# Adding a half-deep third chunk to the seven-product gate and up strips of a two-layer decoder kernel

## The chip, the cores and the metric

The kernel runs on one core of a Trainium2 chip. The metric is device time in microseconds (us) of one execution, lower is better. Engines are named as the profile names them: PE is TensorE (matrix products), DVE is VectorE, ACT is ScalarE, POOL is GpSimd, SP is the engine whose queue issues the transfers.

## The reference, cut to what matters

Two decoder layers on 256 tokens of width 2048, all in 32-bit floats. The change touches the feed-forward part of each layer, with `h` of 256 x 2048 and gate and up weights of 2048 x 5632:

```
h = rms_norm(x, pre_ffn_gain[i])
f = (jax.nn.silu(h @ w_ffn_gate[i]) * (h @ w_ffn_up[i])) @ w_ffn_down[i]
x = x + rms_norm(f, post_ffn_gain[i])
```

## The kernel before, in words

Every product with a weight matrix is made exact enough by splitting both factors into a high and a low part: weights arrive as "raw" chunks `wr` of 256 rows x 512 columns (tile 128x2x512, 512 KB), ACT casts a chunk to its high part `wh` (line 305), DVE subtracts to get the low part `wl` (line 315), and PE does three matmuls of 128x512 for each 128 rows and each 128 tokens: activation high and low against `wh`, activation high against `wl` (lines 404, 407, 408, in function `acc`). There are two token blocks, so one chunk feeds 2 x 2 x 3 = 12 matmuls. The pool of `wh` and `wl` has 7 tiles of each kind, the pool of raw chunks 10. A tile is given out again when its last reader is done.

A strip is 512 output columns, eight chunks deep (2048 rows). The gate strip and the up strip of the same columns are computed together in `paired`. For the first two chunks `fast` treats the two token blocks by the two chunks by the two strips as a 2 x 2 by 2 x 2 block product and forms it from seven products instead of eight (Winograd's variant of Strassen's scheme), with sums of activation blocks made once in a layer (`mixed`) and differences of weight chunks made on DVE in place (line 420). The running sums sit in PSUM tiles: `u` (a tile of the pool `ms`), `c`, `e`, `a` and `d` (`accc`, `acce`, `acca`, `accd`). In the order of the program the seven products are: `u` with chunk r11, then a copy of `u` to SBUF; `c`; `e` with r21; `a`; after the first plain chunk `second` adds to `u`; after the last plain chunk of the gate strip `third` adds to `c` and to `u`. The other six chunks of each strip follow as `plain` chunks: six of gate into `e` and `a`, then six of up into `c` and `d`. When a strip is done DVE adds the saved pieces (lines 381 and 452), ACT takes Silu, DVE multiplies (line 1145), transposes 32x32 blocks (line 251) and the result goes through DRAM to come back turned, after which it is split into `ck` tiles (lines 203 and 204).

Each layer has eleven gate and up strip pairs, numbered n = 0 to 10. The pair n = 0 runs as two ordinary strips, the ten others through `paired`, so there are twenty such pairs in the program. They alternate with the down products in groups of 2, 3, 3 and 3 hidden strips: pairs n = 1 and 2, down group 0, n = 3 and 4, down group 1, n = 5 to 7, down group 2, n = 8 to 10, down group 3. A down pair also goes through `paired`, with four chunks (group 0) or six. Before each down group `mixed` makes sums of the hidden activations (lines 367 and 373).

Each engine executes its instructions in the order that a scheduler fixed when the program was built; a tile's slot and every wait are fixed then too.

Of the kernel before, what the change touches and what calls it, by code (L numbers as in the profile page):

```python
# [15 lines left out]
P = 128  # L16
SEQ = 256
NT = 2
# [29 lines left out]
def decoder(ctx: ExitStack, tc: tile.TileContext, x, p, positions, w_in, attn_sinks,  # L48
# [18 lines left out]
    def tiny(n):  # L67
        return sm.tile([P, n], F32, tag="tiny", name="tiny", bufs=16)
# [4 lines left out]
    def later(n, fn):  # L73

        queue.append((clock[0] + n, fn))
# [19 lines left out]
    def tick():  # L95
        clock[0] += 1
        for gen in list(running):
            if next(gen, True):
                running.remove(gen)
        for item in [q for q in queue if q[0] <= clock[0]]:  # L100
            queue.remove(item)
            item[1]()

    def nat(shape=(P, W), dt=F32):
        return np_.tile(list(shape), dt, tag="nat", name="nat")
# [35 lines left out]
    G.memset(mhalf, -0.5)  # L141


    g0rows = cp.tile([32, P], F32, name="g0rows")
    S.dma_start(g0rows, pre_mix_gain.rearrange("l (c p) -> (l c) p", p=P))
    gT = cp.tile([P, P], F32, name="gT")
    busy = bank()
# [6 lines left out]
    T.transpose(ps[:, 0:32], g0rows, ident[0:32, 0:32])  # L154
    S.preload_act_table(AF.Copy)
    first = V.tensor_copy(gT[:, 0:32], ps[:, 0:32])
    grows = cp.tile([96, P], F32, name="grows")
    lrows = cp.tile([16, P], F32, name="lrows")
    lbl = cp.tile([P, DEPTH, 8], F32, name="lbl")

    at = 0
# [135 lines left out]
    def fetch_w(w, c, col):  # L297
        raw = wpr.tile([P, 2, W], F32, tag="wr", name="wr")
        nc.sync.dma_start(raw, w[c * 2 * P:(c + 1) * 2 * P, col:col + W].rearrange(
            "(k p) n -> p k n", p=P))  # L300
        return raw
# [54 lines left out]
    def mixed(lhs, tags=None):  # L356
# [18 lines left out]
            split(s[i], out[0][i], out[1][i])  # L375
        return lambda i: lambda k: tuple(a[(i - 1) // 2][:, (i - 1) % 2, k] for a in out)

    def summed(done):

        def both(t, ps, x):  # L380
            V.tensor_tensor(x, ps, x, op=ALU.add)
            done(t, x)
        return both

    def paired(lhs, sums, wa, wb, cols, done_a, done_b, nch=8, row0=0, skews=(0, 0),
               after=None, mixed_order=False):

        base = row0 // (2 * P)
        opened = {}

        def psum(name):
            return pacc.tile([P, W], F32, tag="acc", name=name)

        def block(c, t):
            def get(k):
                kt = 2 * c + k
                return tuple(a[:, kt % 4, t * P:(t + 1) * P] for a in lhs[kt // 4])
            return get

        def acc(ps, x, hl):  # L400
            hi, lo = hl
            for k in range(2):
                xh, xl = x(k)
                T.matmul(ps, xh, hi[:, k], start=id(ps) not in opened, stop=False,  # L404
                         skip_group_check=True)
                opened[id(ps)] = ps
                T.matmul(ps, xl, hi[:, k], start=False, stop=False, skip_group_check=True)  # L407
                marks["pe"] = T.matmul(ps, xh, lo[:, k], start=False, stop=k == 1,  # L408
                                       skip_group_check=True)

        def saved(ps):
            b = nat()
            S.copy(b, ps)
            return b

        def parts(r):
            return load_w(None, 0, 0, raw=r)

        def sub(dst, p, q):
            V.tensor_tensor(dst, p, q, op=ALU.subtract)  # L420

        def fast():
            mix = sums()
            r11, r12 = fetch_w(wa, base, cols[0]), fetch_w(wb, base, cols[1])
            r21, r22 = fetch_w(wa, base + 1, cols[0]), fetch_w(wb, base + 1, cols[1])
            u = bank()
            acc(u, block(0, 0), parts(r11))
            x = [saved(u)]
            sub(r11, r12, r11)
            c = psum("accc")  # L430
            acc(c, mix(1), parts(r11))
            p5 = saved(c)
            tick()
            e = psum("acce")
            acc(e, block(1, 0), parts(r21))
            sub(r11, r22, r11)
            sub(r21, r21, r11)
            a = psum("acca")
            acc(a, block(1, 1), parts(r21))
            tick()  # L440
            sub(r12, r22, r12)
            y = []

            def second():
                acc(u, mix(2), parts(r11))
                y.append(saved(u))

            def third():
                acc(c, mix(4), parts(r22))
                acc(u, mix(3), parts(r12))  # L450
                x.append(saved(u))
                V.tensor_tensor(p5, u, p5, op=ALU.add)
                y.append(p5)
                tick()
            return e, a, c, x, y, second, third

        def plain(w, col, banks, skew, end, c0=2, c1=nch, then=None):
            n = c1 - c0
            ws = {}
            for i in range(n + skew):  # L460
                if i < n:
                    ws[i] = load_w(w, base + c0 + i, col)
                    acc(banks[0], block(c0 + i, 0), ws[i])
                    if i == n - 1 and end:
                        end(0)
                if i >= skew:
                    acc(banks[1], block(c0 + i - skew, 1), ws[i - skew])
                if then and i == 0:
                    then()
                tick()  # L470
            if end:
                end(1)

        e, a, c, x1, x2, second, third = fast()

        def end_a(t):
            done_a(t, (e, a)[t], x1[t])

        def end_b(t):
            done_b(t, (c, d)[t], x2[t])  # L480
        if mixed_order:
            plain(wa, cols[0], (e, a), 0, None, c1=nch - 2, then=second)
            third()
            d = psum("accd")
            plain(wb, cols[1], (c, d), 0, None, c1=nch - 2)
            plain(wa, cols[0], (e, a), 0, end_a, c0=nch - 2)
            plain(wb, cols[1], (c, d), 0, end_b, c0=nch - 2)
            return
        def then():
            second()  # L490
            if after:
                after[0]()
        plain(wa, cols[0], (e, a), skews[0], lambda t: t or end_a(t), then=then)
        third()
        end_a(1)
        if after:
            after[1]()
        d = psum("accd")
        plain(wb, cols[1], (c, d), skews[1], end_b)
# [51 lines left out]
    sink = cp.tile([P, DEPTH, 16], F32, name="sink")  # L551
    nsink = cp.tile([P, DEPTH, 16], F32, name="nsink")
    posi = sm.tile([P, NT], I32, name="posi")
    ang = cp.tile([P, NT, 32], F32, name="ang")
    rn, rm, ra, rb = (cp.tile([P, NT, 32], F32, name=f"rope{i}") for i in range(4))
    sin = cp.tile([P, NT, 32], F32, name="sin")
    cos = cp.tile([P, NT, 32], F32, name="cos")

    def constants():
# [51 lines left out]


        G.dma_start(posi, positions.rearrange("o (t p) -> p (o t)", p=P))
        posf = tiny(NT)
        V.tensor_copy(posf, posi)
        for i, f in enumerate(INV_FREQ):
# [87 lines left out]
    for l in range(DEPTH):  # L704
# [427 lines left out]
        def gated(n, last, first):  # L1132
            col = n * W
            gate = {}

            def done_gate(t, ps):
                gate[t] = nat()
                S.activation(gate[t], ps, AF.Silu, scale=rx2(t)[:, 0:1])

            hl = new_ck()  # L1140
            hidden.append(hl)
            wait = 3 if last else 6

            def done_up(t, ps):
                V.scalar_tensor_tensor(gate[t], ps, rx2(t)[:, 0:1], gate[t],
                                       op0=ALU.mult, op1=ALU.mult)
                d = shuffled(gate[t], slow=False)
                later(wait, lambda: split_shuffled(d, None, hl, t))

            if n == 0:  # L1150
                strip(xT, w_ffn_gate[l], col, done_gate, skew=SKEW)
                sx.append(mixed(xT[0], ("kv", "at")))
                later(4, lambda: sx.append(leave_x()))
                strip(xT, w_ffn_up[l], col, done_up)
                return
            if last:
                later(8, lambda: hx.append(mixed(first)))
            paired(xT, lambda: sx[0], w_ffn_gate[l], w_ffn_up[l], (col, col), summed(done_gate),
                   summed(done_up))

        for gi, glen in enumerate(FF_GROUPS):

# [10 lines left out]
            for s in range(4):  # L1173
# [16 lines left out]
                        if s == 3:  # L1190
                            post_norm(macc, ssf, t, nss, nxT, gain_cols(64, l, 16), (4, 3)[t])
                if last and s == 2:
                    fetch_x(sx[1])
                    pT2 = sp.tile([P, 2, 2, SEQ], F32R, tag="at", name="pT2")
                    pT = [pT2[:, 0], pT2[:, 1]]
                    for t in range(NT):
                        pn = nat()
                        nc.sync.dma_start(pn[:, 0:256], p[l, 0, t * P:(t + 1) * P, :])
                        split_T([pn[:, 0:P], pn[:, P:2 * P]], None, pT, t)
# [88 lines left out]
```

## Time and profile before

| what | value |
|---|---|
| runs of the kernel before, us | 2385.58, 2386.97, 2392.02 (median 2386.97) |
| the profiled execution, us | 2387.32 |
| its span, first to last instruction, us | 2385.6 |
| PE busy | 2368.4 us, 99% of the span |
| DVE busy | 1951.8 us, 82% |
| ACT busy | 1373.4 us, 58% |
| mean granted TensorE clock | 0.999 of full speed |

The span is what the trace shows; the time of the execution is 1.7 us more. Busy time is the time in which at least one instruction of the engine was under way. The profile names an instruction by its line in the kernel, its engine, the tile it writes and the tiles it reads.

### The profile page before, as it was taken

How to read it: one execution, taken by the hardware profiler on the slowest of the kernel's cores; microseconds unless marked ns; L12 is line 12 of the kernel's file. 1: busy time of each engine (PE TensorE's matmuls, PEld its weight loads, DVE VectorE, ACT ScalarE, POOL GpSimd, SP SyncE). 2: the span in 40 equal slices, each digit the busy share in tenths (PEclk: the TensorE clock that was granted, in tenths of full speed). 3: DMA queues.
4: the chain of work that ended last, by engine and by line, in shares of the span. 5: the costliest groups of instructions: out<-in, count | busy, mean ns of one | idle time of the engine just before them, and what ended most of it. 6: DMA issues, size and time to landing. Idle time of an engine off the chain costs nothing.

```text
span 2385.6 us, 31637 instructions
## 1 busy us (share of the span) xinstructions
PE 2368.4 (99%) x11011; PEld 1962.8 (82%) x11011; DVE 1951.8 (82%) x2571; ACT 1373.4 (58%) x1958; POOL 105.8 (4%) x213
## 2 busy tenths in 40 slices
PE   9999999999999999999999999999999999999999
PEld 7888887887888888888788888878878888888887
DVE  7787987888897898788777879788888978978885
ACT  6555466556555555556656554665565555555564
POOL 4100001000000000001010000010000000000010
PEclk9999999999999999999999999999999999999999
DMA  8666467667567666766766564676666675676753
GB/s 294 212 194 197 147 211 251 209 213 246 180 220 244 204 229 197 252 215 197 229 218 212 179 215 130 228 256 198 218 212 209 221 247 179 221 235 224 246 164 133
DMA packets 301665, 506.04 MB, mean 212 GB/s; under 512 B 23712, under 2 KB 69696, under 8 KB 301504
## 3 DMA queue, kind: packets, MB, share of 16 engines
q1 hardware_dynamic: 301200, 503.93, 65.0%
q8 instruction: 86, 1.41, 0.2%
q14 instruction: 75, 0.61, 0.1%
q10 hardware_dynamic: 240, 0.07, 0.0%
q0 software_dynamic: 64, 0.02, 0.0%
HBM read 474.57 MB, written 29.36 MB: 211 GB/s over the span
## 4 chain that ended last, share of the span: by engine, by line
PE 93%; DVE 4%; issue 1%; ACT 1%; POOL 1%; DMA 0%; SPq 0%; DVEq 0%; ACTq 0%; POOLq 0%
PE acc L331 9%; PE acc L333 9%; PE acc L330 9%; PE accc L408 5%; PE accc L404 5%; PE accc L407 5%; PE acca L408 5%; PE acca L404 5%; PE acca L407 5%; PE acce L404 5%; PE acce L408 5%; PE acce L407 5%; PE accd L404 4%; PE accd L407 4%; PE accd L408 4%; PE ms L404 2%
## 5 line engine op out<-in xcount | busy, mean ns | idle before, releaser
L305 ACT CAST wh<-wr 128x1024 fp32r<-128x1024 f32 x960 | 991.7, 1052 | 754.9 <-PE acca L407 232.7
L315 DVE TENSOR_TENSOR wl<-wr,wh 128x1024 fp32r<-128x1024 f32 x960 | 1143.9, 1219 | 300.3 <-ACT wh L305 268.6
L330 PE MATMUL acc<-wh,ck 128*128 128x512 f32 x1056 | 417.1, 395 | 0.3 <-ACT ck L203 0.3
L331 PE MATMUL acc<-wh,ck 128*128 128x512 f32 x1056 | 412.4, 391 | 0.3 <-DVE ck L204 0.3
L333 PE MATMUL acc<-wl,ck 128*128 128x512 f32 x1056 | 411.8, 391 | 0.8 <-DVE wl L315 0.8
L333 PEld LDWEIGHTS acc<-wl,ck 128*128 128x128 f32 x1056 | 198.3, 188 | 42.8 <-DVE wl L315 1.7
L331 PEld LDWEIGHTS acc<-wh,ck 128*128 128x128 f32 x1056 | 198.5, 188 | 40.4 <-DVE ck L204 0.7
L330 PEld LDWEIGHTS acc<-wh,ck 128*128 128x128 f32 x1056 | 198.3, 188 | 40.2 <-ACT ck L203 0.7
L420 DVE TENSOR_TENSOR wr<-wr 128x1024 f32<-128x1024 f32 x160 | 194.4, 1220 | 2.4
L404 PE MATMUL acca<-wh,ck 128*128 128x512 f32 x488 | 190.1, 390 | 1.5 <-ACT wh L305 1.5
L404 PE MATMUL acce<-wh,ck 128*128 128x512 f32 x488 | 190.6, 391 | 0.4 <-ACT wh L305 0.4
L408 PE MATMUL acca<-wl,ck 128*128 128x512 f32 x488 | 190.1, 390 | 0.3 <-DVE wl L315 0.3
L408 PE MATMUL acce<-wl,ck 128*128 128x512 f32 x488 | 189.9, 389 | 0.0
L407 PE MATMUL acce<-wh,ck 128*128 128x512 f32 x488 | 189.9, 389 | 0.0
L407 PE MATMUL acca<-wh,ck 128*128 128x512 f32 x488 | 189.9, 389 | 0.0
L404 PE MATMUL accd<-wh,ck 128*128 128x512 f32 x408 | 159.1, 390 | 0.0
L408 PE MATMUL accd<-wl,ck 128*128 128x512 f32 x408 | 158.8, 389 | 0.0
L407 PE MATMUL accd<-wh,ck 128*128 128x512 f32 x408 | 158.7, 389 | 0.0
L407 PE MATMUL accc<-wh,ck 128*128 128x512 f32 x408 | 158.7, 389 | 0.0
L408 PE MATMUL accc<-wl,ck 128*128 128x512 f32 x408 | 158.7, 389 | 0.0
L404 PE MATMUL accc<-wh,ck 128*128 128x512 f32 x408 | 158.7, 389 | 0.0
L404 PEld LDWEIGHTS acca<-wh,ck 128*128 128x128 f32 x488 | 91.6, 188 | 21.1 <-ACT wh L305 2.3
(275 smaller groups left out, 3222.6 us busy)
## 6 DMA issues: line engine op xcount, KB each, us to landing
wr<-in_w_in_dram SPq DMA_DIRECT2D x176, 512.0 KB, 4.8
wr<-in_w_ffn_gate_dram SPq DMA_DIRECT2D x176, 512.0 KB, 5.7
wr<-in_w_ffn_up_dram SPq DMA_DIRECT2D x176, 512.0 KB, 5.2
wr<-in_w_ffn_down_dram SPq DMA_DIRECT2D x176, 512.0 KB, 6.2
wr<-in_w_out_dram SPq DMA_DIRECT2D x64, 512.0 KB, 4.8
wr<-in_w_ple_gate_dram SPq DMA_DIRECT2D x64, 512.0 KB, 5.3
turn<-nat SPq DMA_DIRECT2D x86, 256.0 KB, 2.6
nat<-turn SPq DMA_DIRECT2D x344, 64.0 KB, 3.3
```

The lines of the kernel that those rows point to most:

```text
L305: marks["hi"] = S.copy(hi, raw)
L315: marks["lo"] = V.tensor_tensor(lo, raw, hi.bitcast(F32), op=ALU.subtract)
L330: T.matmul(ps[t], xh, hi[:, k], start=first, stop=False)
L331: T.matmul(ps[t], xl, hi[:, k], start=False, stop=False)
L333: marks[t, c] = marks["pe"] = T.matmul(ps[t], xh, lo[:, k], start=False, stop=last)
L404: T.matmul(ps, xh, hi[:, k], start=id(ps) not in opened, stop=False, skip_group_check=True)
L407: T.matmul(ps, xl, hi[:, k], start=False, stop=False, skip_group_check=True)
L408: marks["pe"] = T.matmul(ps, xh, lo[:, k], start=False, stop=k == 1, skip_group_check=True)
L420: V.tensor_tensor(dst, p, q, op=ALU.subtract)
```

## The change

In the twenty gate and up pairs the third chunk of both strips leaves the plain part. Its two blocks of 128 rows, the two token blocks and the two strips form a second 2 x 2 by 2 x 2 block product, with blocks half as deep, and its seven products are added to the same running sums right behind the seven of the first two chunks. `mixed_half` makes the four sums of activations for it once in a layer (between the gate strip and the up strip of n = 0). The raw chunks are `g` (gate) and `p` (up). `gx` is the split of `g` as it comes, used in `u` and in `e`; one half of `g - p` is split alone (`split_one`) and used in `c`; `g24` is the split of `g` after two more differences, used in `a` and later in `u` (in `second`); `p32` is the split of `p` after one difference, used in `c` and `u` (in `third`). The new sums take the tags `ax` and `ay` of the pool `sp`; eight small tiles of the start of the program (gain rows, rotary working tables) move into the pool `nat`.

```
+    def mixed_half(x):
+        hi = sp.tile([P, 4, 1, P], F32R, tag="ax", name="sum")
+        lo = sp.tile([P, 4, 1, P], F32R, tag="ay", name="sum")
+        full = nat((P, 2, SEQ))
+        V.tensor_tensor(full, x[0][:, 0:2].bitcast(F32), x[1][:, 0:2].bitcast(F32), op=ALU.add)
+        a11, a21, a12, a22 = (full[:, k, t * P:(t + 1) * P] for k in range(2) for t in range(NT))
+        s = nat((P, 4, 1, P))
+        for i, p, q, op in ((0, a21, a22, ALU.add), (1, s[:, 0, 0], a11, ALU.subtract),
+                            (2, a11, a21, ALU.subtract), (3, a12, s[:, 1, 0], ALU.subtract)):
+            V.tensor_tensor(s[:, i, 0], p, q, op=op)
+        split(s, hi, lo)
+        return lambda i: lambda k: (hi[:, i - 1, 0], lo[:, i - 1, 0])
...
+        def split_one(r, k):
+            hi = wps.tile([P, 2, W], F32R, tag="wh", name="wh")
+            lo = wps.tile([P, 2, W], F32R, tag="wl", name="wl")
+            split(r[:, k], hi[:, k], lo[:, k])
+            return hi, lo
...
             r11, r12 = fetch_w(wa, base, cols[0]), fetch_w(wb, base, cols[1])
+            if half:
+                more = half()
+                g, p = fetch_w(wa, base + 2, cols[0]), fetch_w(wb, base + 2, cols[1])
             r21, r22 = fetch_w(wa, base + 1, cols[0]), fetch_w(wb, base + 1, cols[1])
             u = bank()
             acc(u, block(0, 0), parts(r11))
+            if half:
+                gx = parts(g)
+                acc(u, block(2, 0), gx, (0,))
             x = [saved(u)]
             sub(r11, r12, r11)
             c = psum("accc")
             acc(c, mix(1), parts(r11))
+            if half:
+                sub(g[:, 0], p[:, 0], g[:, 0])
+                acc(c, more(1), split_one(g, 0), (0,))
             p5 = saved(c)
             tick()
             e = psum("acce")
             acc(e, block(1, 0), parts(r21))
+            if half:
+                acc(e, block(2, 0), gx, (1,))
             sub(r11, r22, r11)
             sub(r21, r21, r11)
             a = psum("acca")
             acc(a, block(1, 1), parts(r21))
+            if half:
+                sub(g[:, 0], p[:, 1], g[:, 0])
+                sub(g[:, 1], g[:, 1], g[:, 0])
+                g24 = parts(g)
+                acc(a, block(2, 1), g24, (1,))
+                sub(p[:, 0], p[:, 1], p[:, 0])
             tick()
             sub(r12, r22, r12)
...
             def second():
                 acc(u, mix(2), parts(r11))
+                if half:
+                    acc(u, more(2), g24, (0,))
...
             def third():
                 acc(c, mix(4), parts(r22))
+                if half:
+                    p32 = parts(p)
+                    acc(c, more(4), p32, (1,))
                 acc(u, mix(3), parts(r12))
+                if half:
+                    acc(u, more(3), p32, (0,))
...
-        def plain(w, col, banks, skew, end, c0=2, c1=nch, then=None):
+        def plain(w, col, banks, skew, end, c0=head, c1=nch, then=None):
```

The first place is DVE's queue where one gate and up pair follows another (n = 6 to n = 7, and every pair that follows a pair). `wr<-wr` is a difference of raw chunks, `wl<-wr,wh` a split, `nat<-accc` and `nat<-accd` the two additions that close the up strip of the pair before; the second of them waits for the last matmul of that pair. Before:

```order
L420 TENSOR_TENSOR wr<-wr 128x1024 x2
L315 TENSOR_TENSOR wl<-wr,wh 128x1024 x2
L420 TENSOR_TENSOR wr<-wr 128x1024 x2
L315 TENSOR_TENSOR wl<-wr,wh 128x1024 x3
L381 TENSOR_TENSOR nat<-accc,nat 128x512
L381 TENSOR_TENSOR nat<-accd,nat 128x512
```

And now, from the split of `gx` on:

```order
L315 TENSOR_TENSOR wl<-wr,wh 128x1024
L434 TENSOR_TENSOR wr<-wr 128x1024
L434 TENSOR_TENSOR wr<-wr 128x512
L434 TENSOR_TENSOR wr<-wr 128x1024
L315 TENSOR_TENSOR wl<-wr,wh 128x1024
L204 TENSOR_TENSOR wl<-wr,wh 128x512
L434 TENSOR_TENSOR wr<-wr 128x1024
L315 TENSOR_TENSOR wl<-wr,wh 128x1024
L434 TENSOR_TENSOR wr<-wr 128x512
L434 TENSOR_TENSOR wr<-wr 128x1024
L395 TENSOR_TENSOR nat<-accc,nat 128x512
L434 TENSOR_TENSOR wr<-wr 128x512
```

Behind these rows now stand the Silu product, the addition of `accd`, a transpose and another product, and only then the splits for `a` and `g24`; before, the split for `a` and two later ones stood ahead of both additions.

The second place is DVE's queue where the pair n = 3 follows the short down group 0; `macc_5156` (before) and `macc_5181` (now) are the last output strip of that group. Before:

```order
L1182 TENSOR_TENSOR macc_5156<-accc,nat 128x512
L420 TENSOR_TENSOR wr<-wr 128x1024
L1182 TENSOR_TENSOR macc_5156<-accd,nat 128x512
L420 TENSOR_TENSOR wr<-wr 128x1024 x2
L315 TENSOR_TENSOR wl<-wr,wh 128x1024 x14
```

Now:

```order
L1229 TENSOR_TENSOR macc_5181<-accc,nat 128x512
L434 TENSOR_TENSOR wr<-wr 128x512
L434 TENSOR_TENSOR wr<-wr 128x1024
L1229 TENSOR_TENSOR macc_5181<-accd,nat 128x512
L204 TENSOR_TENSOR wl<-wr,wh 128x512
L315 TENSOR_TENSOR wl<-wr,wh 128x1024
L434 TENSOR_TENSOR wr<-wr 128x512
L434 TENSOR_TENSOR wr<-wr 128x1024
L434 TENSOR_TENSOR wr<-wr 128x512 x2
L315 TENSOR_TENSOR wl<-wr,wh 128x1024 x2
L434 TENSOR_TENSOR wr<-wr 128x1024
L315 TENSOR_TENSOR wl<-wr,wh 128x1024 x12
```

Behind the addition of `accd` the split for `a` (the first of the two in `x2`) now has four half differences, one full difference, a half split and a full split ahead of it; before, it stood behind two full differences.

## Rows read from the trace of the kernel before

**Rows 1.** The page's part on busy time, share of the span and instructions.

```profile
span 2385.6 us, 31637 instructions
PE 2368.4 (99%) x11011; PEld 1962.8 (82%) x11011; DVE 1951.8 (82%) x2571; ACT 1373.4 (58%) x1958; POOL 105.8 (4%) x213
```

**Rows 2.** The page's chain of work that ended last, by engine.

```profile
PE 93%; DVE 4%; issue 1%; ACT 1%; POOL 1%; DMA 0%; SPq 0%; DVEq 0%; ACTq 0%; POOLq 0%
```

**Rows 3.** All waits of PE, first layer's pairs and down groups: total, times, longest.

```profile
PE acca L404 <- ACT wh L305: 0.6, 1, 0.6
PE acce L404 <- ACT wh L305: 0.2, 1, 0.2
PE acca L408 <- DVE wl L315: 0.2, 1, 0.2
```

**Rows 4.** PE in order of time: start, duration, instruction, twelve matmuls apart.

```profile
604.91 0.39 PE L404 MATMUL accc<-wh,ck 128*128 128x512 f32 x1
...
607.63 0.39 PE L404 MATMUL ms<-wh,ck 128*128 128x512 f32 x1
```

**Rows 5.** Stretches: length, busy time of PE, PEld, DVE, ACT, POOL, clock, DMA.

```profile
522.09:564.33 42.24, 41.42 (x181) 33.56 (x180) 40.40 (x43) 24.36 (x29) 0.00 (x0) 1.00 0.68 224
564.33:606.95 42.62, 42.45 (x187) 34.84 (x186) 36.33 (x34) 25.21 (x28) 0.00 (x0) 1.00 0.62 212
...
649.79:712.45 62.66, 62.66 (x277) 51.73 (x276) 57.67 (x61) 35.10 (x41) 0.00 (x0) 1.00 0.63 218
...
754.61:796.77 42.16, 42.16 (x187) 34.91 (x186) 33.99 (x35) 24.11 (x28) 0.00 (x0) 1.00 0.70 224
```

**Rows 6.** Groups of instructions by line and shape: busy, mean ns, idle before.

```profile
L315 DVE TENSOR_TENSOR wl<-wr,wh 128x1024 fp32r<-128x1024 f32 x960 | 1143.9, 1219 | 300.3 <-ACT wh L305 268.6 <-PE ms L408 22.1 <-DMA nat<-turn 3.0
L305 ACT CAST wh<-wr 128x1024 fp32r<-128x1024 f32 x960 | 991.7, 1052 | 754.9 <-PE acca L407 232.7 <-DVE wr L420 196.5 <-PE acc L331 158.4
...
L204 DVE TENSOR_TENSOR ck<-nat,ck 128x512 fp32r<-128x512 f32 x52 | 35.7, 686 | 1.6 <-ACT ck L203 1.4
L203 ACT CAST ck<-nat 128x512 fp32r<-128x512 f32 x52 | 32.2, 619 | 8.8 <-DMA nat<-turn 4.2 <-DVE nat L215 3.9
...
L373 DVE TENSOR_TENSOR nat<-nat 128x256 f32<-128x256 f32 x56 | 21.5, 419 | 0.1
```

**Rows 7.** DVE in order of time, end of pair n = 6, start of n = 7.

```profile
782.62 0.68 DVE L381 TENSOR_TENSOR nat<-acca,nat 128x512 f32<-128x512 f32 x1
783.22 2.47 DVE L420 TENSOR_TENSOR wr<-wr 128x1024 f32<-128x1024 f32 x2
785.63 2.36 DVE L315 TENSOR_TENSOR wl<-wr,wh 128x1024 fp32r<-128x1024 f32 x2
...
791.58 2.36 DVE L315 TENSOR_TENSOR wl<-wr,wh 128x1024 fp32r<-128x1024 f32 x2 [1.20 <-ACT wh L305]
...
796.90 1.40 DVE L1145 SCALAR_TENSOR_TENSOR nat<-nat,ry 128x512 f32<-128x512 f32 x2
798.22 0.70 DVE L251 STREAM_TRANSPOSE nat<-nat 128x512 f32<-128x512 f32 x1
798.85 2.32 DVE L315 TENSOR_TENSOR wl<-wr,wh 128x1024 fp32r<-128x1024 f32 x2
```

**Rows 8.** DVE in order of time, down group 0 and start of n = 3.

```profile
519.80 1.23 DVE L315 TENSOR_TENSOR wl<-wr,wh 128x1024 fp32r<-128x1024 f32 x1 [1.17 <-ACT wh L305]
...
522.29 0.69 DVE L381 TENSOR_TENSOR nat<-accd,nat 128x512 f32<-128x512 f32 x1 [0.66 <-PE accd L408]
...
547.39 8.04 DVE L315 TENSOR_TENSOR wl<-wr,wh 128x1024 fp32r<-128x1024 f32 x7 [1.17 <-ACT wh L305]
...
567.91 1.23 DVE L315 TENSOR_TENSOR wl<-wr,wh 128x1024 fp32r<-128x1024 f32 x1
569.35 12.70 DVE L315 TENSOR_TENSOR wl<-wr,wh 128x1024 fp32r<-128x1024 f32 x11 [0.20 <-ACT wh L305]
583.53 1.23 DVE L315 TENSOR_TENSOR wl<-wr,wh 128x1024 fp32r<-128x1024 f32 x1 [1.49 <-ACT wh L305]
```

More of the change, by code (lines that the diff above doesn't have):

```diff
@@ L141, in decoder @@
     G.memset(mhalf, -0.5)
-    g0rows = cp.tile([32, P], F32, name="g0rows")
+    g0rows = nat()[0:32, 0:P]
     S.dma_start(g0rows, pre_mix_gain.rearrange("l (c p) -> (l c) p", p=P))
@@ L156, in decoder @@
     first = V.tensor_copy(gT[:, 0:32], ps[:, 0:32])
-    grows = cp.tile([96, P], F32, name="grows")
-    lrows = cp.tile([16, P], F32, name="lrows")
+    grows = nat()[0:96, 0:P]
+    lrows = nat()[0:16, 0:P]
     lbl = cp.tile([P, DEPTH, 8], F32, name="lbl")
@@ L385, in paired @@
     def paired(lhs, sums, wa, wb, cols, done_a, done_b, nch=8, row0=0, skews=(0, 0),
-               after=None, mixed_order=False):
+               after=None, mixed_order=False, half=None):
         base = row0 // (2 * P)
@@ L398, in block, with acc @@
             return get
-        def acc(ps, x, hl):
+        def acc(ps, x, hl, ks=(0, 1)):
             hi, lo = hl
-            for k in range(2):
+            for k in ks:
                 xh, xl = x(k)
@@ L407, in acc @@
                 T.matmul(ps, xl, hi[:, k], start=False, stop=False, skip_group_check=True)
-                marks["pe"] = T.matmul(ps, xh, lo[:, k], start=False, stop=k == 1,
+                marks["pe"] = T.matmul(ps, xh, lo[:, k], start=False, stop=k == ks[-1],
                                        skip_group_check=True)
@@ L455, in fast @@
             return e, a, c, x, y, second, third
-        def plain(w, col, banks, skew, end, c0=2, c1=nch, then=None):
+        head = 3 if half else 2
+        def plain(w, col, banks, skew, end, c0=head, c1=nch, then=None):
             n = c1 - c0
@@ L553, in decoder @@
     posi = sm.tile([P, NT], I32, name="posi")
-    ang = cp.tile([P, NT, 32], F32, name="ang")
-    rn, rm, ra, rb = (cp.tile([P, NT, 32], F32, name=f"rope{i}") for i in range(4))
     sin = cp.tile([P, NT, 32], F32, name="sin")
@@ L613, in constants @@
         G.dma_start(posi, positions.rearrange("o (t p) -> p (o t)", p=P))
+        work = nat((P, 5, NT, 32))
+        ang, rn, rm, ra, rb = (work[:, i] for i in range(5))
         posf = tiny(NT)
@@ L1152, in gated @@
                 sx.append(mixed(xT[0], ("kv", "at")))
+                sx.append(mixed_half(xT[1]))
                 later(4, lambda: sx.append(leave_x()))
@@ L1158, in gated @@
             paired(xT, lambda: sx[0], w_ffn_gate[l], w_ffn_up[l], (col, col), summed(done_gate),
-                   summed(done_up))
+                   summed(done_up), half=lambda: sx[1])
         for gi, glen in enumerate(FF_GROUPS):
```

2 lines of the change are left out of this document (1 added, 1 removed).

## Prediction

> **What bounds the kernel now.** I read the page first: PE is busy 99% of the span, DVE 82%, ACT 58% [rows 1], and the chain that ended last is 93% PE [rows 2]. So a matmul that goes away shortens the run, unless PE then waits for something else. What a matmul costs is read from starts, since their durations overlap: twelve take 2.72 us, 604.91 to 607.63, or 0.2267 us each [rows 4]. The stretches confirm it: the pair n = 6 has 7 x 2 x 3 + 6 x 4 x 6 = 186 matmuls and takes 42.16 us, 186 x 0.2267 [rows 5]. The granted clock is 1.00 in all of these stretches, the 2.4 GHz level.
>
> The waits say where PE is not solid: in the first layer's pairs and down groups there are three, 1.0 us in all, each for a cast or a split [rows 3]. The stretches say where: down group 0 has 2 x 90 matmuls, 40.80 us, and takes 42.24; n = 3 behind it takes 42.62 for 42.16 [rows 5]. That is 1.9 us lost, and there DVE is busy 40.40 of 42.24 us. In an ordinary pair such as n = 6 DVE is busy 33.99 of 42.16 us. So PE is the bound nearly everywhere, DVE in one stretch of each layer, and the change takes from the first and gives to the second.
>
> **What goes away.** The third chunks of a pair cost 2 x 12 = 24 matmuls; the new products cost 7 x 3 = 21. Twenty pairs lose 3 each: 60 x 0.2267 = 13.6 us. Nothing else on PE changes but the order.
>
> The Trainium skill, TensorE: Matmul & The Clock Gate, Back-to-back issue gap, gives for 512 columns an isolated gap of 512/2.4 + 2.5 = 216 ns, and about 131 ns sustained in a stream of weight loads and matmuls. By these the saving would be an estimated 13.0 or 7.9 us. The trace here shows 226.7 ns in exactly such a stream, so I stay with the row.
>
> **What is added on DVE and ACT.** A full split takes 1.15 us of DVE's queue (eleven in 12.70 [rows 8]), a full difference 1.20 (two, 783.22 to 785.63), an operation of 512 columns 0.60 (782.62 to 783.22), a Silu product 0.66, a transpose 0.63 [rows 7]. The two splits that leave are replaced by three full ones and a half one, and there are four half differences: 1.15 + 0.60 + 4 x 0.60 = 4.2 us more in each pair. The half split has no row; its nearest is the split of 128x512 on L204, 686 ns alone [rows 6], and back to back it should lie between 0.60 and 0.69. In the shape of n = 6, DVE then has about 38.2 of 41.5 us. ACT gets a full and a half cast, 1.05 + 0.62 us [rows 6], on 24.11 [rows 5], and does not become the bound. The chunks fetched stay 16 a pair; p and g are held longer, but the fetches stand far ahead in SP's queue and I price them at nothing (uncovered, one late chunk would cost a few us in a pair).
>
> DVE has idle time in sum, so what matters is whether it has it at the right moment: `fast` now needs its splits close together, and each `wh` and `wl` tile of the seven waits for PE to finish with an older one.
>
> **A pair behind a pair** (n = 2, 4, 6, 7, 9, 10, twelve in all). I count from the start of the pair before on PE, in which the last products of `third` end after 36 + 60 + 9 + 18 = 123 matmuls, 27.9 us. The first split of the next pair waits for one of the tiles used there, free at about 27. Cast 1.05, split 1.15, two additions 0.60 each: DVE reaches `gx` at 30.4. From there to the first plain split the new order holds six full splits (6.9), a half one (0.6), four full differences (4.8), four half ones (2.4), two additions (1.2), two Silu products (1.3) and two transposes (1.3): 18.5, so 48.9. PE wants that low part at 41.5 (183 matmuls) + 36 matmuls + the two that use the high part: 50.1. It is early by 1.2 us. The split for `a`, at 45.4, is needed at 48.0. So these pairs cost nothing beyond the saving, with 1.2 us to spare; in rows 7 the same split stood at 791.58, ahead of the end of the pair. The casts lie in the shadow of differences: between every difference and the split that needs it another one stands.
>
> **Behind a down group of six chunks** (n = 5, 8) I take nothing. Down group 1 takes 62.66 us for 2 x 138 matmuls, 62.57, so PE loses nothing there, and DVE idles 5.0 us of it [rows 5]. What the new order adds ahead of `a` (`gx`, the half split, four half differences, 4.2) less the nine matmuls by which `a` is wanted later (2.04) is 2.1, less than that.
>
> **Behind down group 0** (n = 3, once a layer) DVE has no reserve. In rows 8 it runs from the addition of `accd` at 522.29 to the split for `a` ending at 569.14 all but without a gap: the one row above half a us is 1.17, the latency of a cast. Between these two points the new order adds: the split for the down pair's `a`, which stood ahead of the addition (519.80) and now stands behind it, 1.15; `gx` 1.15; the half split 0.60; four half differences 2.4; less the full difference for r12, now behind `a`, 1.20. Sum 4.1. PE wants `a` nine matmuls later, 2.04. So PE waits 2.1 us more at `a`. Behind it DVE does `g24`, that difference and the first plain split, 3.5 us, while PE has 13 matmuls, 2.95: 0.5 more, less what n = 3 lost already at this place before (some 0.4). I take 2.2 us a layer, 4.4 in all. After that DVE gains on PE again, 1.15 against 2.72 us a chunk, as before in the eleven splits of 12.70 [rows 8].
>
> Bounds for the 4.4: 0 if the lateness is taken up by gaps earlier in the group, 8.2 if all that is added shows twice.
>
> **The small parts.** `mixed_half` is two DVE operations of 512 columns and four of 128, these between nothing and the 0.42 of 256 columns [rows 6]: 1.2 to 2.9 us and a cast, once a layer. It stands among the splits of the up strip of n = 0; without that cover n = 1 would lose up to 2.9 us, but my count has its first plain split 2.8 us early. The tiles moved into `nat` at the start hold no engine; between 1 us gained and 1 lost, I take 0.
>
> **Sum.** 2387.3 - 13.6 + 4.4 = 2378.1 for the profiled execution, which lies 0.35 above the median of its runs, 2386.97. I predict 2378. A measurement of this kernel can tell about 0.3%, 7.2 us, from no change: the edge is 2379.8.
>
> **Rivals.**
> (A) Everything is hidden: DVE's backlog of n = 3 is worked off in time. For it: PE waits only 1.0 us in that layer today [rows 3]. Against it: DVE is already the bound there. 2387.3 - 13.6 = 2373.7, up to 2375.5.
> (B) The twelve pairs behind a pair lose too. The 1.2 us to spare is the difference of two sums of 50 us; if a tile is freed one product later (2 us) the first plain split is about 0.8 us late, in each: 12 x 0.8 = 9.6, and 2378 becomes 2388, no change. For it: DVE's share rises to 92% there. Against: DVE idles 8 us in such a pair now, and less lateness (0.3 us) makes only 2382.
> (C) Slower. `gx`, `g24` and `p32` hold tiles over two products each, so only five or six of seven are left for running ahead. If that makes the split chain begin behind the last product of `third` instead of beside it, it starts some 4 us later (18 matmuls) and each of the twelve pairs loses 4 - 1.2 = 2.8 us: 34 us, 2412. It decides from a lateness of 1.2 + 9.2/12 = 2.0 us on; slower by 0.3% needs 2.6. Against: in rows 7 two of the splits of the next pair stand complete well ahead of the pair's end.
> The Trainium skill, Perfetto Trace Analysis, Identifying the Most-Contended Engine, speaks for (C): it reads TensorE by its weight loads, here 82%, and VectorE by its busy time, here also 82%, so that work moved between them would gain nothing. The chain at 93% PE does not agree with that.
> (D) The products saved don't shorten the run, since PE is limited at those places by its feeding anyway: 2385 to 2388. Against: 42.16 us for 186 matmuls at the plain spacing.
>
> **How the numbers follow.** Forecast (2375.5 to 2380.5) 0.50, A 0.14, B 0.22, C 0.07, D 0.07. The range reaches from A's 2373.5 to B's upper end, 2387, which leaves out C and a little of the rest. Faster by over 0.3%: A, and most of the forecast, 0.42: 0.56. Slower: C, 0.07. The rest, 0.37, within 0.3%.
>
> **What would show it.** Right: pairs such as n = 6 take 41.5 us (183 matmuls), with no wait of PE above 0.2; n = 3 and down group 0 together take about 86.4 us instead of 84.9, with a wait at `acca` for its low part; DVE busy about 2040 us. Wrong: waits of PE at the first plain chunk or at `a` in every pair (B, C), or pairs of 41.5 us in n = 3 too (A).

## The result and the profile after

| | before | after |
|---|---|---|
| median, us | 2387.64 (2385.58 to 2392.02, 5 runs) | 2378.72 (2377.57 to 2380.66, 5 runs) |
| profiled execution, us | 2387.32 | 2380.66 |
| its span, us | 2385.6 | 2378.9 |
| DVE busy, us | 1951.8 | 2026.5 |

The ratio is 0.9961, with a 95% interval from 0.9947 to 0.9976: 8.9 us less, and the forecast was 2378. The profiled execution of after is the longest of its five, 1.9 us above their median, so stretches are compared below and not spans.

The page of after, the parts that answer to [rows 1] and [rows 2]:

```profile
span 2378.9 us, 31721 instructions
PE 2358.3 (99%) x10951; PEld 1950.6 (82%) x10951; DVE 2026.5 (85%) x2703; ACT 1398.0 (59%) x2000; POOL 106.6 (4%) x213
...
PE 92%; DVE 4%; issue 1%; DMA 1%; ACT 1%; POOL 1%; SPq 0%; DVEq 0%; ACTq 0%; POOLq 0%
```

PE executes 60 matmuls fewer and still rules the chain. The stretches of after that answer to [rows 5] (length, busy time and instructions of PE, PEld, DVE, ACT, POOL, clock, DMA): down group 0, n = 3, down group 1, n = 6.

```profile
521.87:564.99 43.12, 41.60 (x182) 33.48 (x181) 41.66 (x45) 26.75 (x32) 0.00 (x0) 1.00 0.68 219
564.99:608.27 43.28, 42.36 (x184) 34.11 (x183) 39.94 (x42) 26.39 (x30) 0.00 (x0) 1.00 0.55 195
649.75:712.66 62.91, 62.91 (x277) 51.57 (x276) 59.94 (x65) 36.56 (x42) 0.00 (x0) 1.00 0.64 217
754.14:795.62 41.48, 41.48 (x184) 34.35 (x183) 37.50 (x41) 25.41 (x30) 0.00 (x0) 1.00 0.68 228
```

The pair n = 6 went from 42.16 to 41.48 us, which is 183 x 0.2267; so did every gate and up pair but n = 3 (n = 1 had 42.26). Down group 0 got 0.88 us longer, and n = 3, with three matmuls fewer, 0.66 us longer. Down group 1 got 0.25 longer, in its first down pair; so did group 2 (31.38 to 31.62 us for that pair), and group 3 got 0.27 longer.

All waits of PE in the first layer's pairs and down groups, as in [rows 3]:

```profile
PE acca L418 <- ACT wh L305: 1.5, 2, 1.3
PE acca L422 <- DVE wl L315: 0.5, 1, 0.5
PE acce L418 <- ACT wh L305: 0.2, 1, 0.2
```

The longest, 1.3 us, lies in the second down pair of group 0, where 0.6 stood before; the other two at `acca` lie in n = 3. A wait that is listed costs more than its number: the next matmuls start 0.34 us apart and not 0.23. By the starts on PE, n = 3 lost 0.44 us before and loses 1.74 now; group 0 lost 1.4 and loses 2.25.

### The profile page after: what moved, and what is told of

It is laid out like the page before. It is cut to its first block, busy times and chain, and to the rows that moved or that the text cites. A ratio compares the mean times of both kernels' runs of the same rounds, so it can differ in the third digit from the quotient of the medians.

```text
span 2378.9 us, 31721 instructions
## 1 busy us (share of the span) xinstructions
PE 2358.3 (99%) x10951; PEld 1950.6 (82%) x10951; DVE 2026.5 (85%) x2703; ACT 1398.0 (59%) x2000; POOL 106.6 (4%) x213
## 4 chain that ended last, share of the span: by engine, by line
PE 92%; DVE 4%; issue 1%; DMA 1%; ACT 1%; POOL 1%; SPq 0%; DVEq 0%; ACTq 0%; POOLq 0%
PE acc L331 9%; PE acc L330 9%; PE acc L333 9%; PE accc L418 5%; PE accc L421 5%; PE accc L422 5%; PE acca L422 4%; PE acce L422 4%; PE acce L418 4%; PE acca L418 4%; PE acca L421 4%; PE acce L421 4%; PE accd L422 3%; PE accd L418 3%; PE accd L421 3%; PE ms L418 3%
## 5 line engine op out<-in xcount | busy, mean ns | idle before, releaser
L305 ACT CAST wh<-wr 128x1024 fp32r<-128x1024 f32 x980 | 1006.0, 1051 | 722.9 <-DVE wr L434 209.3
L315 DVE TENSOR_TENSOR wl<-wr,wh 128x1024 fp32r<-128x1024 f32 x980 | 1163.0, 1217 | 212.7 <-ACT wh L305 204.9
L434 DVE TENSOR_TENSOR wr<-wr 128x1024 f32<-128x1024 f32 (+1 forms) x240 | 243.8, 1038 | 0.8
L418 PE MATMUL acca<-wh,ck 128*128 128x512 f32 x468 | 182.6, 390 | 3.1 <-ACT wh L305 3.1
L422 PE MATMUL acca<-wl,ck 128*128 128x512 f32 x468 | 182.3, 390 | 1.1 <-DVE wl L315 1.1
L418 PE MATMUL acce<-wh,ck 128*128 128x512 f32 x468 | 182.7, 390 | 0.4 <-ACT wh L305 0.4
L421 PE MATMUL acce<-wh,ck 128*128 128x512 f32 x468 | 182.1, 389 | 0.0
L421 PE MATMUL acca<-wh,ck 128*128 128x512 f32 x468 | 182.1, 389 | 0.0
L422 PE MATMUL accd<-wl,ck 128*128 128x512 f32 x368 | 144.7, 393 | 0.0
L418 PE MATMUL accd<-wh,ck 128*128 128x512 f32 x368 | 143.7, 390 | 0.0
L421 PE MATMUL accd<-wh,ck 128*128 128x512 f32 x368 | 143.2, 389 | 0.0
L421 PE MATMUL accc<-wh,ck 128*128 128x512 f32 x368 | 143.2, 389 | 0.0
L422 PE MATMUL accc<-wl,ck 128*128 128x512 f32 x368 | 143.2, 389 | 0.0
L418 PE MATMUL accc<-wh,ck 128*128 128x512 f32 x368 | 143.1, 389 | 0.0
```

The costliest lines, as they stand in the source:

```text
L305: marks["hi"] = S.copy(hi, raw)
L315: marks["lo"] = V.tensor_tensor(lo, raw, hi.bitcast(F32), op=ALU.subtract)
```

## The experiments

The stretch of one layer is given unless both differ; unless said otherwise the numbers to hold a kernel against are those of after, 41.48 us a pair, 43.12 for down group 0, 43.28 for n = 3.

**n = 3 in its old form** (the third chunk of this pair as a plain chunk again).

```
-                   summed(done_up), half=lambda: sx[1])
+                   summed(done_up), half=None if n == 3 else lambda: sx[1])
```

> The changed kernel with the pair n = 3 of each layer in its old form (third chunk as a plain chunk, 186 matmuls); the other eighteen pairs keep the new products. My theory (n = 3 waits because DVE's queue behind down group 0 has 4.2 us more to do): the two waits at `acca`, 1.8 us a layer, fall back to about 0.5, and down group 0 and n = 3 together go from 86.4 us to 84.9, so the whole is about 3 us shorter than the changed kernel, 2375.7 us. Rival (the stall has another cause, such as tiles of the seven that come free late, or the way that group 0 ends): the six matmuls come back with nothing for them, 86.4 + 0.7 = 87.1 us, the whole 1.4 us longer, 2380.1.

2377.37 us (2376.3 to 2378.24). Its second layer, down group 0 and n = 3, and the second down pair of group 0 of its first layer:

```profile
542.60:566.02 23.42, 21.91 (x88) 17.30 (x87) 20.47 (x22) 12.89 (x15) 0.00 (x0) 0.93 0.55 193
1702.17:1745.34 43.17, 41.70 (x182) 33.47 (x181) 41.70 (x45) 26.72 (x32) 0.00 (x0) 1.00 0.65 219
1745.34:1787.99 42.65, 42.48 (x187) 34.84 (x186) 37.54 (x38) 24.91 (x28) 0.00 (x0) 1.00 0.58 198
```

Half of the expectation held. The gaps of n = 3 fell to 0.44 us, the value of before, although its three matmuls came back; but group 0 kept its 43.17, so the two take 85.82 and not 84.9. What group 0 lost does not come from n = 3. (The first layer's down pair, 23.42 us where the other layer has 21.79, is a fall of the clock; see the end.)

**n = 2 in its old form** (`half=None if n == 2`, the same line).

> The changed kernel with the pair n = 2 of each layer (the one ahead of down group 0) in its old form. Theory: DVE is the bound from the end of n = 2 on, and the first down pair of group 0, 21.3 us against 20.5 before, pays for work that n = 2 in its new form pushes behind it. Then this pair goes back to 20.5 us, n = 2 takes 42.2 instead of 41.5, n = 3 keeps its 43.3, and the whole is 2378.4, 0.3 us less than the changed kernel. Rival (the 0.8 us comes from what n = 3 in its new form asks of DVE or of the transfers during the group): the first down pair stays at 21.3, the whole is 2380.1.

2379.97 us, one run. The stretches of n = 2, down group 0 and n = 3, and then the waits of PE in the group:

```profile
480.81:522.97 42.16, 42.16 (x188) 34.91 (x186) 36.44 (x42) 25.17 (x29) 0.00 (x0) 1.00 0.67 224
522.97:565.24 42.27, 41.46 (x181) 33.55 (x180) 40.39 (x43) 24.40 (x29) 0.00 (x0) 1.00 0.67 224
565.24:608.54 43.30, 42.35 (x185) 34.12 (x184) 39.96 (x42) 26.38 (x30) 0.00 (x0) 1.00 0.56 195
```

```profile
PE acca L418 <- ACT wh L305: 0.6, 1, 0.6
PE acce L418 <- ACT wh L305: 0.2, 1, 0.2
```

Group 0 is back at 42.27 us and its wait at 0.6, with n = 3 still at 43.30. (Most of the loss, 0.7 of 0.85 us, lies in the second down pair; the 21.3 us of the expectation hold three matmuls of that pair, which the changed kernel starts early.) DVE is busy 1.27 us less in the group (40.39 for 41.66): that is the split for the first down pair's `a`, which the new form of n = 2 pushes behind the group's start. The single time does not show it (it lies at the rival's 2380.1), since the gain in the group, 0.85 us a layer, is nearly what the three matmuls of n = 2 cost, 0.68.

**Both in their old form** (`half=None if n in (2, 3)`).

> The changed kernel with both pairs around down group 0, n = 2 and n = 3 of each layer, in their old form; the sixteen other pairs keep the new products. From the two runs with one of them in its old form: with n = 2 old, the wait in the second down pair of group 0 falls from 1.3 to 0.6 us; with n = 3 old, its own gaps fall from 1.8 to 0.45. If the two are independent, n = 2, down group 0 and n = 3 together take 42.16 + 42.27 + 42.62 = 127.05 us, against 127.88 in the changed kernel and 127.22 with n = 3 alone in its old form; the whole is 1.7 us under the changed kernel, 2377.0. Rival (they share one backlog, so that one of the two is enough): 127.9 us, and the whole as the changed kernel or longer, 2378.7 to 2380.

2376.69 us (2375.45 to 2379.53), ratio to before 0.9959 [0.9945, 0.9972].

```profile
478.98:521.13 42.15, 42.15 (x187) 34.91 (x186) 36.44 (x42) 25.16 (x29) 0.00 (x0) 1.00 0.68 224
521.13:563.41 42.28, 41.47 (x182) 33.55 (x180) 40.41 (x43) 24.33 (x29) 0.00 (x0) 1.00 0.67 224
563.41:606.03 42.62, 42.45 (x188) 34.83 (x186) 37.55 (x38) 24.88 (x28) 0.00 (x0) 1.00 0.57 198
```

127.05 us in each layer, to a hundredth what the two single edits add up to: the two losses are independent, and around down group 0 the new products cost more than they save. This version has the lowest median of those that leave nothing out; against the changed kernel the 2 us are under what times can tell apart, and the stretches, 0.83 us a layer, carry the verdict.

**n = 3 without its half differences** (the four `sub` of half blocks left out for n = 3, so that chunk is multiplied with the blocks as they come).

> The changed kernel without the four half differences of the pair n = 3, so that its third chunk is multiplied with the raw blocks instead (that part of the result is left out); every split and every matmul stays. It takes 2.4 us off DVE's queue ahead of the first plain split and puts nothing in its place. Theory (DVE's queue is what n = 3 waits for): its 1.8 us of waits go to 0.5 or less, 41.5 to 42.0 us instead of 43.3, the whole 3 us less, 2375.5 to 2376. Rival (what it waits for is the chain of a cast and a split behind each difference, or tiles that come free late): 43 us or more.

2376.84 us (2376.3 to 2379.67); n = 3 takes 42.74 us. The expectation missed: 2.4 us off DVE's queue gave 0.54. DVE and ACT at the start of n = 3 (564.39), first here, then in the kernel after (n = 3 starts at 564.99):

```profile
565.58 0.69 DVE L1233 TENSOR_TENSOR macc<-accd,nat 128x512 f32<-128x512 f32 x1
566.18 3.49 DVE L434 TENSOR_TENSOR wr<-wr 128x1024 f32<-128x1024 f32 x3
570.83 6.90 DVE L315 TENSOR_TENSOR wl<-wr,wh 128x1024 fp32r<-128x1024 f32 x6 [1.17 <-ACT wh L305]
...
569.75 7.69 ACT L305 CAST wh<-wr 128x1024 fp32r<-128x1024 f32 x8 [0.49 <-DVE wr L434]
```

```profile
568.50 3.02 DVE L434 TENSOR_TENSOR wr<-wr 128x512 f32<-128x512 f32 x4
571.50 2.36 DVE L315 TENSOR_TENSOR wl<-wr,wh 128x1024 fp32r<-128x1024 f32 x2
573.77 1.22 DVE L434 TENSOR_TENSOR wr<-wr 128x1024 f32<-128x1024 f32 x1
...
570.41 6.74 ACT L305 CAST wh<-wr 128x1024 fp32r<-128x1024 f32 x7 [0.56 <-DVE wr L434]
```

The scheduler filled the place: three full differences in a row now stand ahead of the cast for `a`, which starts when the last of them ends (569.67). The one too many is that for r12, which after has behind the cast (573.77). The cast starts 5.36 us into the pair, as against 5.42. And two of the half differences had cost nothing in after: they ran while DVE would have waited 1.17 us for that cast.

**n = 3 without the difference for r12 as well** (five differences left out in all).

> The changed kernel in which the pair n = 3 leaves out its four half differences and the full difference for r12 (the products then take the chunks as they are; that part of the result is left out). In the run without the half differences alone, the scheduler put the difference for r12 in the place that came free, ahead of the cast for `a`, and that cast stood 5.36 us after the start of n = 3 as against 5.42 in the changed kernel. Now only the two differences that `a` needs stand there. Theory (what n = 3 waits for at `a` is what stands in DVE's queue ahead of the cast for `a`): the cast comes 1.15 us earlier, the wait at `a` (1.2 us with its low part) goes to 0.1 or less, n = 3 takes 41.5 to 41.7 us. Rival (the wait is the chain of difference, cast and split itself, or tiles that come free late): 42.4 us or more again.

2376.51 us, one run; n = 3 takes 42.17 us. DVE and ACT:

```profile
565.30 2.48 DVE L434 TENSOR_TENSOR wr<-wr 128x1024 f32<-128x1024 f32 x2
569.36 11.44 DVE L315 TENSOR_TENSOR wl<-wr,wh 128x1024 fp32r<-128x1024 f32 x10 [1.58 <-ACT wh L305]
...
567.79 0.59 ACT L427 COPY nat<-accc 128x512 f32<-128x512 f32 x1 [1.45 <-PE accc L422]
568.27 9.60 ACT L305 CAST wh<-wr 128x1024 fp32r<-128x1024 f32 x10
```

Another 0.57 us went, between the two theories. The difference that `a` needs was done at 567.78, but the cast waited half a us behind a copy on ACT, which itself waited for PE's product `c`. So of the 1.74 us of n = 3 some 1.1 go with DVE's differences, and 0.65 are the chain of cast and split with ACT's order in it. How the 1.1 divide between the half differences and the full one can't be read from these two runs, since the order changed between them.

**n = 3's half differences on GpSimd** (`G.tensor_tensor` in their place).

> The changed kernel with the four half differences of the pair n = 3 on GpSimd in place of DVE (2.4 us off DVE's queue ahead of the first plain split). My theory (DVE's queue is the bound there): the stall of n = 3 falls from 1.8 us to 0.5 or less, down group 0 and n = 3 together from 86.4 to 84.2 to 85.0 us, the whole about 3 us a program shorter than the changed kernel, 2375.5. Rival (the transfer to GpSimd costs as much as it saves, because its operation takes much longer than 0.6 us and the split behind it waits for it, or slows DVE meanwhile): 86.4 or more, the whole 2378.7 to 2382.

2384.04 us (2381.55 to 2386.97); n = 3 takes 44.54 us, 1.26 more. Three of the four half differences on GpSimd, and operations of DVE beside them, each row by itself:

```profile
562.75 2.32 POOL L437 TENSOR_TENSOR wr<-wr 128x512 f32<-128x512 f32 x1
565.70 2.22 POOL L437 TENSOR_TENSOR wr<-wr 128x512 f32<-128x512 f32 x1 [0.63 <-DVE wl L204]
568.00 2.15 POOL L437 TENSOR_TENSOR wr<-wr 128x512 f32<-128x512 f32 x1
```

```profile
562.69 1.23 DVE L315 TENSOR_TENSOR wl<-wr,wh 128x1024 fp32r<-128x1024 f32 x1
567.28 1.72 DVE L434 TENSOR_TENSOR wr<-wr 128x1024 f32<-128x1024 f32 x1
568.92 2.31 DVE L434 TENSOR_TENSOR wr<-wr 128x1024 f32<-128x1024 f32 x1
571.15 1.21 DVE L434 TENSOR_TENSOR wr<-wr 128x1024 f32<-128x1024 f32 x1
```

The rival was right, by the second of its two reasons: no split waits for GpSimd here, but DVE is slowed. (The time lies above the rival's range too; see the end.) A half difference takes 2.2 to 2.3 us there, 0.60 on DVE; and two full differences of DVE that ran meanwhile took 1.72 and 2.31 us in place of 1.2. So 2.4 us of DVE's work were bought with 1.6 us of slower work. The rows show the two engines taking turns: the half difference that starts just behind the split of 562.69 ends 1.15 us after that split (563.92 and 565.07), and each of the two slow differences ends 1.08 us after the half difference that was under way when it started (567.92 and 569.00, 570.15 and 571.23). So about half of the 2.3 us on GpSimd is waiting. The Trainium skill, SBUF — State Buffer, section SBUF: two separate sides, has an exclusive lock between a DVE operation with two SBUF inputs and a GpSimd operation that reads SBUF. The trace agrees with that in these ends; the addition from PSUM in that stretch kept its 0.68 us. And here too the difference for r12 came ahead of the cast for `a`, as one of three full ones; the cast starts 7.14 us into the pair (572.45) and not 5.42.

**n = 3's half product for `c` behind `a`** (the three lines of `c` moved behind `acc(a, block(1, 1), ...)` for n = 3; nothing is left out).

> The changed kernel in which the pair n = 3 makes its half-deep product for `c` behind the full product for `a` instead of ahead of `e`; the result is the reference's. On DVE the half split for it then stands behind the split for `a`, and 1.2 us less of DVE's work stands between the addition of the last `accc` and the cast for `a` (4.65 us instead of 5.85 by the durations of the trace). Theory: the wait of 1.2 us at `a` goes to 0.3 or less, n = 3 takes 42.0 to 42.3 us instead of 43.3, down group 0 is unchanged, the whole is about 2 us less, 2376.5. Rival (the same work only waits at the next place): the gaps move to the first plain chunk or to `g24` and n = 3 stays at 43.0 or more, 2378.

2384.92 us (2381.7 to 2387.48): a miss, and slower than after. The gaps of n = 3 rose to 4.4 and 3.3 us. ACT, and PE behind it in the first layer:

```profile
573.34 0.59 ACT L427 COPY nat<-accc 128x512 f32<-128x512 f32 x1 [2.72 <-PE accc L422]
573.96 7.72 ACT L305 CAST wh<-wr 128x1024 fp32r<-128x1024 f32 x8
```

```profile
575.06 0.80 PE L418 MATMUL acca<-wh,ck 128*128 128x512 f32 x1 [1.76 <-ACT wh L305]
...
577.45 0.63 PE L418 MATMUL acca<-wh,ck 128*128 128x512 f32 x1
577.88 0.63 PE L421 MATMUL acca<-wh,ck 128*128 128x512 f32 x1
```

The wait moved, as the rival had it, and grew: the copy of `c` now waits for the late product, and all casts, that of `g24` first, wait behind it on ACT. I had counted DVE's queue and not ACT's.

**A probe ahead of `g24`** in the twelve pairs behind a pair: `V.tensor_tensor(g, g, g, op=ALU.max)`, twice.

> The changed kernel with two more full operations on DVE (the maximum of `g` with itself, 1.20 us each, 2.4 in all) ahead of the split of `g24`, in the twelve pairs that follow a pair. It measures how much DVE has to spare there. My count of 1.2 us to spare: each of these pairs goes from 41.5 to 42.7 us, 14 us in all, 2393. Nothing to spare (the range's upper end): 43.9 us each, 29 us, 2408. More than 2.4 us to spare (my count left out gaps that DVE can fill): no change, 2378.7, and the pairs stay at 41.5.

2400.89 us, one run; these pairs take 43.46 us, 1.98 more. It doesn't measure the reserve, since the operations stand in the chain of `g24` itself: PE waits 0.88 us there, for its cast.

**A probe that no product waits for** (the same on `p`, behind its last difference).

> The changed kernel with more full operations on DVE (the maximum of `p` with itself, which no product needs before the up strip) right ahead of the first plain split in the twelve pairs that follow a pair: one (about 1.15 us) in the first layer, two in the second. The trace of the changed kernel has that split end 1.3 us before PE wants it. Theory (DVE's order sets the time, 1.2 to 1.3 us to spare, as predicted): the pairs of the first layer stay at 41.5 us, those of the second go to about 42.5; 2378.7 + 6 x 1.0 = 2384.7. Rival (the tiles held over two products leave less to spare than that, 0.4 us as a first reading of the other probe would have it): 42.2 and 43.4, the whole 2394. Third case (later splits catch it up and nothing shows): 2378.7.

2380.75 us, one run. A pair of the first layer, one of the second:

```profile
606.89:648.42 41.53, 41.53 (x185) 34.27 (x183) 38.56 (x45) 24.14 (x30) 0.00 (x0) 1.00 0.65 228
1789.19:1830.93 41.74, 41.74 (x185) 34.20 (x183) 39.69 (x46) 23.93 (x30) 0.00 (x0) 1.00 0.66 227
```

One operation costs 0.05 us at most, two cost about 0.26 us a pair and not 1.0. DVE in the second layer (the two operations are those of L478):

```profile
1795.32 1.18 DVE L478 TENSOR_TENSOR wr<-wr 128x1024 f32<-128x1024 f32 x1
1796.42 1.22 DVE L315 TENSOR_TENSOR wl<-wr,wh 128x1024 fp32r<-128x1024 f32 x1
1797.55 1.22 DVE L478 TENSOR_TENSOR wr<-wr 128x1024 f32<-128x1024 f32 x1
```

The two do not stand together: the scheduler put the first plain split between them, so that only one of them delays it. That split ends at 1797.64, and its matmul starts at 1797.80. On PE the high parts of the second plain chunk for both token blocks now stand ahead of its first low part, and the 0.26 us are lost there. So the reserve of the first plain split is the one operation, 1.10 us, and these 0.16, about as counted (1.2); what two operations ahead of it would cost was not measured. A probe can change what it measures.

**Six tiles instead of seven**, after and before (`bufs=6` in the pool of `wh` and `wl`).

> The changed kernel with six tiles of `wh` and of `wl` instead of seven; nothing else. Theory (DVE's order sets the time, the ring of tiles has some room left): the pairs stay at 41.5 us or lose less than 0.3, n = 3 and down group 0 together stay near 86.4. Rival (the ring is what binds, as in the case C of the prediction, since `gx`, `g24` and `p32` hold tiles over two products): with one fewer each pair that follows a pair loses 1 to 3 us, 2390 to 2415 in all.

> The kernel before with six tiles of `wh` and `wl` instead of seven. It is to be held against the changed kernel with six, which lost 37 us, 2.6 us of it in each down pair that follows a gate and up pair and only 0.36 in a pair that follows a pair. Theory (the change, by holding three more tiles over two products each, has used up the seventh tile at those places): before loses less than 10 us, 2390 to 2397, and its first down pairs stay within 0.5 us of 31.4. Rival (these places needed the seventh tile already): 2415 to 2425, first down pairs of 33 us or more.

One run each: 2415.66 and 2392.98 us. The first down pair of group 1, first after, then before, each with six:

```profile
656.03:690.31 34.28, 32.55 (x140) 25.43 (x139) 32.27 (x35) 19.64 (x23) 0.00 (x0) 1.00 0.62 215
```

```profile
651.50:682.88 31.38, 31.38 (x140) 25.82 (x138) 29.22 (x32) 16.76 (x21) 0.00 (x0) 1.00 0.71 234
```

Before needs the seventh tile little (6.2 us), after loses 37 us without it. The pairs behind a pair lose only 0.36 us each, so the ring is not what sets their time; down pairs behind a gate and up pair lose 2.65. The change has used up the seventh tile there.

**Only the moved tiles of the start**, nothing else of the change.

> The kernel before with only the eight small tiles of the start moved into the pool `nat`, nothing else of the change. My theory: no engine's work moves, 2387.6 us, and the work ahead of the first pairs ends at the same time as before (the first matmul into `ms` of n = 1 within 0.3 us). Rival: these tiles wait in turn for the pool's other readers, which explains why the changed kernel's pairs begin 1.2 us later: 2388.8.

2387.43 us (2385.88 to 2388.98), ratio 0.9999 [0.999, 1.0009]: nothing. The `w_out` pair ahead of n = 0 begins at 304.44 us here and at 303.09 in before, with the same time of the whole, and anywhere from 302.8 to 304.8 in the other profiles. The 1.2 us by which after begins it later is the spread of single executions. A part of that spread can be seen: in the profiles of after and of this run the granted clock is 0.96 over the first 10 us and 0.87 and 0.86 over the next 10, in that of before 1.00 in both. Of the five profiles that begin later than 304.1 these two and two more show such a fall and one (304.60) does not; of those that begin earlier none does.

## Why the prediction was right

| step | forecast, us | measured in the stretches, us |
|---|---|---|
| 60 matmuls | -13.6 | -13.6 (0.68 in each pair) |
| twelve pairs behind a pair | 0 | 0 |
| n = 3 and down group 0, two layers | +4.4 | +4.2 |
| first down pairs of groups 1 and 2 (four), group 3 | 0 | +1.5 |
| `mixed_half`, moved tiles | 0 | 0 |
| sum | -9.2 | -7.9; medians -8.9 |

The 1.0 us between the last two figures lies within the spread of single executions.

**The matmuls** were sized by the starts on PE, and 41.48 us for 183 confirms 0.2267 each.

**Pairs behind a pair** went as counted. The count had the first plain split done 48.9 us after the start of the pair before, and wanted at 50.1. The rows of n = 6 to n = 7 (start of n = 6 at 754.14), DVE from the split of `gx` on and PE:

```profile
784.79 1.22 DVE L315 TENSOR_TENSOR wl<-wr,wh 128x1024 fp32r<-128x1024 f32 x1
...
801.76 5.72 DVE L315 TENSOR_TENSOR wl<-wr,wh 128x1024 fp32r<-128x1024 f32 x5
```

```profile
804.24 0.39 PE L422 MATMUL acce<-wl,ck 128*128 128x512 f32 x1
```

DVE reaches `gx` 30.65 us after the start (30.4 counted) and has no gap from there on. The first of the five ends at 802.9, 48.8 us after the start, and its matmul starts at 50.1. None of these twelve pairs shows a wait.

**n = 3 and down group 0**: 86.40 us, as forecast (86.4), but the 2.2 us a layer were put in one place and lie in two. n = 3 loses 1.3 us more than before; 0.85 are lost in the group, 0.7 of them in its second down pair, and they come from n = 2, which I had priced at nothing. (In the second layer the kernel before already loses 0.3 us more there, so that the two layers make 4.2 and not 4.4.) The step that failed is that "these pairs cost nothing beyond the saving": true where a pair follows, not where down group 0 does. The sum fits in part because both are the same count: the split for the down pair's `a`, 1.15 us behind its place, was in it, and DVE has no gap until n = 3 to lose it in but the 1.17 us that it waits for a cast at 548.02. The rest is luck: 1.15 were counted for that split and 0.85 lost, 1.05 for n = 3 itself and 1.3 lost, and the two errors cancel. Nor does the count name the last wait rightly everywhere: at `a` of n = 3 PE waits 0.25 us for the cast and 0.53 for the split, and what is left when DVE's extra work is gone, 0.65 us, is ACT's order and the chain itself.

**Smaller misses.** The first down pairs of groups 1 to 3 lose about 0.25 us each, unforecast. In group 1 PE's starts lie 0.30 to 0.33 us apart there at three places (661.61, 663.35, 666.63), at one in before; no wait is listed for them, and the cause stays open. DVE's busy time rose by 75 us and not by 88. By the starts in the trace, each operation counted up to the start of the next, the twenty full splits more cost 18.7 us where 23 were counted, and the 160 full differences, which now stand closer behind other work, went from 190.3 to 184.2.

**The rivals.** A (all hidden, 2373.7) fell with n = 3. B and D fell with 41.48 us in every steady pair. C's mechanism is real but one tile away: with seven it shows nothing in the pairs behind a pair, with six the changed kernel loses 37 us and the kernel before 6, most of it at the down pairs rather than where C had it. The rule of the Trainium skill, Perfetto Trace Analysis, Identifying the Most-Contended Engine, that was cited for it would, as the prediction read it, have had no gain from the trade; the trace had the gain at PE's own spacing, and DVE's 37.50 of 41.48 us did not matter.

## What to carry to other kernels

A matmul saved is worth its spacing wherever the stretch is solid on PE; price the work it costs on another engine stretch by stretch, where that engine has no gap, and follow it past the stretch in which it was added, since it shows at the next place that can't wait. Try such a trade with a switch for each place: here the pairs on both sides of the one short group are better left alone, and 16 of 20 bring all of the gain. Leaving an operation out to measure it works only if what the scheduler puts in its place is read first, on each engine with a queue in the chain.

## What was not expected of the hardware

After a wait of PE the granted clock sometimes falls to the lower of its two levels (1.2 GHz) for some matmuls. In the rows of the run with the late product for `c`, behind a wait of 1.76 us, matmuls start 0.43 us apart (577.45, 577.88) and not 0.23, and the view by stretches gives it as

```profile
575.00:580.00 5.00, 4.94 (x15) 3.73 (x16) 4.96 (x5) 5.00 (x7) 0.00 (x0) 0.66 0.49 147
```

The same wait in the second layer of that run brought no fall. One of 1.3 us brought one in one layer of the first experiment (clock 0.93 there, 23.42 us for 21.79) and none in the changed kernel. Between the two layers PE waits 1.9 us in before and 2.2 in after, and the clock over 1150 to 1165 is 0.89 in both; in the run with the moved tiles alone it waits 2.7 us there, and the clock stays at 1.00. So the length of the wait alone does not decide it in these runs.

A fall costs 1.1 us in the run with the late product and 1.6 us in the first experiment. It is a part of the spread between executions of one kernel, and probably of why the two kernels with waits of 2 us in n = 3 came out 5 to 6 us above after when their stretches account for 2.5 and 4.3. The mean granted clock of the single executions fits that: with the half differences on GpSimd it was 0.998 to 1.000 in the six that took 2381.55 to 2384.1 us, and 0.996 to 0.997 in the four that took 2386.53 to 2386.97. Where in those executions the clock fell is not shown.
